# V's seven products in another order, with their gate words on VectorE and x's combination back on SyncE's queue

## The chip, the cores and the metric

The kernel runs on one core of one Trainium2 chip. What is measured is the device time of one execution in microseconds (us). Five engines work side by side, each through its own list of instructions in order: TensorE (PE, matrix products; PEld are its weight loads), VectorE (DVE), ScalarE (ACT), GpSimd (POOL) and SyncE (SP, which here only issues transfers). Transfers between the chip's main memory (HBM) and the on-chip memory (SBUF) can be issued by SyncE, ScalarE or GpSimd and are carried out by 16 DMA engines. TensorE adds its results up in PSUM, which has 8 banks. An engine that needs another's result waits at the head of its list, and everything behind it in that list waits too.

## The reference

One decoder block with 512 tokens and 2048 features: a norm, one wide input projection, attention in two groups of heads, an output projection, and a last norm. What matters here is the projection of the values of group A and of the 24 gate columns:

```python
h = _rmsnorm(x, norm_g[l])
proj = h @ w_in[l]
(qa, kca, vca, ksa, vsa, kwa, vwa, za, ga,
 qb, kb, vb, zb) = jnp.split(proj, offsets, axis=-1)
...
kc = _compress(_rope(_heads(kca, N_KV_A, HEAD_DIM_A)), cmp_k_pos[l], cmp_k_w1[l], cmp_k_w2[l])
vc = _compress(_heads(vca, N_KV_A, HEAD_DIM_A), cmp_v_pos[l], cmp_v_w1[l], cmp_v_w2[l])
...
o_sel = _selected_attention(qa, _rope(_heads(ksa, N_KV_A, HEAD_DIM_A)), _heads(vsa, N_KV_A, HEAD_DIM_A), sel_idx)
o_win = _banded_attention(qa, _rope(_heads(kwa, N_KV_A, HEAD_DIM_A)), _heads(vwa, N_KV_A, HEAD_DIM_A), WIN_A)
gates = jax.nn.sigmoid(ga.astype(jnp.float32)).reshape(B, S, N_KV_A, GROUP_A, 3).astype(x.dtype)
```

`vsa` and `vwa` are 256 columns each: together they are what the kernel calls V. `_compress` squeezes blocks of 32 tokens through two small matrices, once for keys and once for values.

## The kernel before

**Words.** Products are taken in a fast 32-bit format that keeps fewer bits. So every operand is split in two words: ScalarE copies it into the high word, VectorE subtracts that from the source to get the low word (`split`, lines 541 and 542). A product of two split operands is three matmuls (`mm3`, lines 119 to 121). The words of weights lie in three rotating buffers (`words`, tags `whi` and `wlo`), so VectorE and ScalarE can be at most three buffers ahead of TensorE.

**Seven products.** x is cut in even and odd blocks of 128 features and in tokens 0 to 255 and 256 to 511; the weights of V in four quarters (0: `vsa` of the even blocks, 1: `vwa` of the even, 2: `vsa` of the odd, 3: `vwa` of the odd). The 2 by 2 block product is then formed with seven products instead of eight, by combinations of x and sums of quarters. Their names and the weights that each uses are: 22 (quarter 3), p (quarter 0), 21 (quarter 1), 12 (quarter 0 + quarter 2), u (quarter 0 + 2 + 3), w (quarter 2 + 3), q (all four). A quarter is held in two halves (g = 0, 1) of 128 x 1024 numbers, 512 KB. The sums are made in place: p's tiles become those of 12, then u, then q; w's own tiles get quarter 3 added.

Of x's combinations, those for p, u and q are kept in SBUF as words (`pu`, `qw`). The one for w is built earlier, written to HBM (`wd`) and brought back over the even blocks of x's first 256 tokens (`even`, lines 825 to 827), four transfers of 512 KB that may start once the last projection before the stage (`proj(wz[19])`) has read those blocks. Only product w reads them; 12 and 22 read the odd blocks, 21 the even blocks of the other tokens.

**The stage.** The order is 22, p, 21, 12, u, w, q. Four of the products are `wide` (22, p, 21, 12): beside 256 value columns they carry the 24 gate columns, whose weights are split too, for two blocks at a time: ScalarE makes the high gate word (line 839), GpSimd the low one (line 840). One wide product is 8 blocks x 2 groups of 128 tokens x 3 matmuls of 280 columns. The other three are `narrow`, with 256 columns. 22 and 21 share one pair of PSUM banks, p and 12 another, u and q a third bank, w a fourth; `vd` and `vj` gather them on VectorE.

Between the halves of these products stand the 16 units of the compression's first matrix (`compress_unit`, line 686 on; 0 to 7 for keys, 8 to 15 for values). Each loads two halves of 256 KB (`cw`, line 696, SyncE's queue) into four small tiles, splits them, and takes 8 matmuls. So SyncE's queue holds the cw loads, the quarters of V, and the first quarters of the stage behind it: `keys(1)`, which takes seven products of the same kind for a pair of keys. Its quarter 0 goes to tile `raw3`, quarter 2 to `raw1` (with quarter 3 added to it by an accumulating transfer on GpSimd, line 907), quarter 3 and the sum of 0 and 2 to the two tiles `quarters` (named `ahead` in the profile), in which 21 and then w lay before, and quarter 1 to `raw2`. Quarter 1 of V is added into u's tiles to make q's by accumulating transfers on GpSimd too (line 910).

`v_words` turns finished rows of V into words: ScalarE's copies, GpSimd's subtractions, and a transfer to HBM on GpSimd's queue. Its small tile `other` uses the slot `pcr`, in which `gw[0]`, one of the two gate weights, lies before.

**What sets the order.** The program text gives priorities; a planner with its own estimate of each instruction's duration takes, for each engine, the earliest instruction in the text that it holds to be ready. The list it writes is fixed. `tc.issue_after(i)` keeps what is inside it behind instruction i on i's engine.

## Time and profile before

| | us |
|---|---|
| median of 3 timed runs | 824.88 |
| lowest and highest of them | 821.97 and 828.35 |
| the profiled execution | 826.33 |
| its span, from the first to the last instruction | 824.5 |
| mean granted TensorE clock in it | 0.986 |

The page gives for each engine its busy time, and the span in 40 slices with the busy share in tenths. A row of the windows view has the window and its length in us, then for each engine the busy time and the number of instructions, then the TensorE clock that was granted (1.00 is full speed), the mean busy share of the 16 DMA engines, and GB/s. A row of the timeline has the start and the duration in us, the engine (SPq is SyncE's queue), the line, the operation with result<-sources and shape, and how many were merged; in brackets is how long the engine stood idle before it and who ended that. A group's row has busy time, mean ns of one, and the idle time before them.

### The profile page before, as it was taken

Reading aid. Unit: us, or ns where it says so; the run is one execution under the profiler, and the core shown is the slowest. Engines: PE = TensorE matmul, PEld = TensorE weight load, DVE = VectorE, ACT = ScalarE, POOL = GpSimd, SP = SyncE. Lnnn points to the kernel's source line nnn. Section 1 sums busy time; section 2 is a strip of 40 time slices with the busy share of each in tenths; the row PEclk is TensorE's granted clock in tenths of the full one; section 3 lists DMA queues with packets and bytes.
Section 4 is the critical chain, followed back from the end, with each engine's and each line's share of the span. In section 5 each row is a group of like instructions: output and inputs, shape, how many; then the busy total and the mean of one; then the engine's idle time right before and its main releaser. Section 6 shows DMA issues by size and latency. Waiting matters only on the chain.

```text
span 824.5 us, 15301 instructions
## 1 busy us (share of the span) xinstructions
PE 797.6 (97%) x5644; PEld 742.4 (90%) x5644; DVE 699.9 (85%) x1399; ACT 512.5 (62%) x1108; POOL 123.6 (15%) x132
## 2 busy tenths in 40 slices
PE   9999999999999969889999999999999999999996
PEld 8887888888888859779999999999999999999996
DVE  7668979988898857856999999998999798977895
ACT  6636656756666436455445796868687877554555
POOL 4515001111011013422111101110100000010000
PEclk9999999999999979989999999999999999999999
DMA  7562144456455465794752232244033935797845
GB/s 245 173 228 91 67 149 133 149 142 193 149 157 167 153 210 175 198 262 119 205 162 70 78 116 69 65 151 132 27 112 119 368 116 205 255 260 182 238 114 204
DMA packets 49595, 132.08 MB, mean 160 GB/s; under 512 B 6033, under 2 KB 9137, under 8 KB 49521
## 3 DMA queue, kind: packets, MB, share of 16 engines
q1 hardware_dynamic: 43088, 110.89, 40.3%
q0 software_dynamic: 6144, 19.70, 10.6%
q8 instruction: 44, 0.72, 0.4%
q10 hardware_dynamic: 288, 0.52, 0.2%
q14 instruction: 31, 0.25, 0.1%
HBM read 114.28 MB, written 16.81 MB: 159 GB/s over the span
## 4 chain that ended last, share of the span: by engine, by line
PE 42%; DVE 9%; DMA 6%; issue 5%; ACT 2%; POOL 0%; POOLq 0%; ACTq 0%; DVEq 0%
PE pj L121 8%; PE pj L119 8%; PE pj L120 7%; PE sp L984 4%; PE oa L120 2%; PE oa L121 2%; PE oa L119 2%; DVE wlo L542 2%; DMA cw<-cw 2%; DMA rw<-wos 2%; DMA ch<-wos 2%; PE tp L1021 2%; PE bank L120 1%; DVE wlo L1104 1%; PE op L1027 1%
## 5 line engine op out<-in xcount | busy, mean ns | idle before, releaser
L119 PE MATMUL pj<-xh,whi 128*128 128x256 f32 (+1 forms) x592 | 197.2, 333 | 0.1
L121 PE MATMUL pj<-xh,wlo 128*128 128x256 f32 (+1 forms) x592 | 196.6, 332 | 0.3 <-DVE wlo L542 0.3
L120 PE MATMUL pj<-xl,whi 128*128 128x256 f32 (+1 forms) x592 | 196.6, 332 | 0.0
L121 PEld LDWEIGHTS pj<-xh,wlo 128*128 128x128 f32 x592 | 111.6, 188 | 10.6 <-DVE wlo L542 0.6
L119 PEld LDWEIGHTS pj<-xh,whi 128*128 128x128 f32 x592 | 111.4, 188 | 10.7 <-ACT t L607 0.5
L120 PEld LDWEIGHTS pj<-xl,whi 128*128 128x128 f32 x592 | 111.4, 188 | 9.6
L541 ACT ACTIVATE whi<-raw 128x1024 fp32r<-128x1024 f32 (+1 forms) x82 | 80.2, 993 | 39.1 <-DVE raw L580 11.6
L542 DVE TENSOR_TENSOR wlo<-raw,whi 128x1024 fp32r<-128x1024 f32 (+1 forms) x82 | 95.9, 1182 | 6.0 <-ACT whi L541 5.6
L99 DVE TENSOR_TENSOR wlo<-raw,whi 128x1024 fp32r<-128x1024 f32 (+1 forms) x60 | 71.4, 1191 | 16.4 <-ACT whi L97 15.9
L97 ACT ACTIVATE whi<-raw 128x1024 fp32r<-128x1024 f32 (+1 forms) x59 | 55.5, 943 | 24.4 <-PE pj L120 13.6
L120 PE MATMUL oa<-wlo,xh 128*128 128x256 f32 x200 | 55.6, 278 | 0.0
L119 PE MATMUL oa<-whi,xh 128*128 128x256 f32 x200 | 55.5, 278 | 0.0
L121 PE MATMUL oa<-whi,xl 128*128 128x256 f32 x200 | 55.3, 277 | 0.0
L121 PE MATMUL pj<-pu,wlo 128*128 128x256 f32 x160 | 45.2, 283 | 0.7 <-DVE wlo L542 0.7
L119 PE MATMUL pj<-pu,whi 128*128 128x256 f32 x160 | 45.3, 283 | 0.0
L120 PE MATMUL pj<-pu,whi 128*128 128x256 f32 x160 | 44.8, 280 | 0.0
L288 ACT ACTIVATE ph<-tp 128x512 fp32r<-128x512 f32 (+1 forms) x64 | 34.2, 562 | 15.2 <-PE tp L384 7.5
L289 DVE TENSOR_TENSOR pl<-tp,ph 128x512 fp32r<-128x512 f32 (+1 forms) x64 | 40.7, 649 | 0.9 <-ACT ph L288 0.7
L121 PEld LDWEIGHTS oa<-whi,xl 128*128 128x128 f32 x200 | 37.6, 188 | 0.0
L120 PEld LDWEIGHTS oa<-wlo,xh 128*128 128x128 f32 x200 | 37.6, 188 | 0.0
L119 PEld LDWEIGHTS oa<-whi,xh 128*128 128x128 f32 x200 | 37.5, 188 | 0.0
L363 ACT ACTIVATE ttb<-ttb,sums 128x256 f32<-128x256 f32 (+1 forms) x64 | 30.0, 471 | 10.8 <-DVE sums L356 10.8
(428 smaller groups left out, 2398.6 us busy)
## 6 DMA issues: line engine op xcount, KB each, us to landing
raw<-wq SPq DMA_DIRECT2D x41, 512.0 KB, 4.0
raw<-wz SPq DMA_DIRECT2D x36, 512.0 KB, 3.7
cw<-cw SPq DMA_DIRECT2D x32, 256.0 KB, 3.7
raw<-wos SPq DMA_DIRECT2D x14, 512.0 KB, 5.8
rw<-wos SPq DMA_DIRECT2D x10, 512.0 KB, 5.4
xr<-xT SPq DMA_DIRECT2D x16, 256.0 KB, 3.6
rows<-xT SPq DMA_DIRECT2D x8, 512.0 KB, 4.4
raw<-wo SPq DMA_DIRECT2D x8, 512.0 KB, 5.8
```

Source lines behind the costliest of these rows:

```text
L97: last["hi"] = act.activation(hi[:, :width], rw[:, :width], AF.Copy).ins
L99: last["lo"] = dve.tensor_tensor(out=lo[:, :width], in0=rw[:, :width], in1=hi[:, :width].bitcast(F32), op=ALU.subtract).ins
L119: pe.matmul(ps, ah, bh, start=first, stop=False, skip_group_check=go_on)
L120: pe.matmul(ps, ah, bl, start=False, stop=False, skip_group_check=go_on)
L121: recent["mm"] = pe.matmul(ps, al, bh, start=False, stop=last, skip_group_check=go_on).ins
L288: act.activation(ph, tp, AF.Copy)
L289: dve.tensor_tensor(out=pl, in0=tp, in1=ph.bitcast(F32), op=ALU.subtract)
L363: act.activation(tv, tv, AF.Exp, bias=mn[:, e, v:v + 1], scale=-1.0, accum_out=dn[:, e, v:v + 1])
L541: split_hi = act.activation(hi, src, AF.Copy).ins
L542: last["lo"] = dve.tensor_tensor(out=lo, in0=src, in1=hi.bitcast(F32), op=ALU.subtract).ins
L984: pe.matmul(sp[:, a:b], qq[:, qs], kk[:, ko:ko + b - a], start=pi == 0, stop=pi == 2)
L1021: pe.transpose(tp[:, e * 256 + i * P:e * 256 + i * P + P], views[2 * i + w][2][:, kt * P:(kt + 1) * P], ident)
```

## The change

The order of the products becomes 22, p, 12, u, 21, w, q. w is loaded into `quarters` at the start, where 21 was; 21 is loaded later, into 22's tiles, once u's and w's sums have read them. The sums for 12 stand behind p, those for u and w behind 12. The two pairs of banks are swapped. The units are spread anew: 6 and 7 in u, 8 and 9 in 21, 10 to 13 in w; 14 and 15 stay in q. The low gate words and the sum of the gate weights go from GpSimd to VectorE. The four transfers that bring x's combination back go from GpSimd's queue to SyncE's, behind p's and w's loads in the text. Of the key pair's quarters, 0 now comes into 22's tile after 21; quarter 2, its accumulate, and the sum stand behind the load of quarter 3, which follows w, and quarter 1 after them.

```diff
-    for ms in (slice(0, 4), slice(4, 8)):
-        for e in range(2):
-            pool.dma_start(even[e][:, ms], wd[e, :, ms])
-    pair22, pair11 = [bank(4), bank(5)], [bank(0), bank(1)]
+    pair22, pair11 = [bank(0), bank(1)], [bank(4), bank(5)]
...
-                pool.tensor_tensor(out=gl, in0=gate[:, m:m + 2, :], in1=gh.bitcast(F32), op=ALU.subtract)
+                dve.tensor_tensor(out=gl, in0=gate[:, m:m + 2, :], in1=gh.bitcast(F32), op=ALU.subtract)
...
     for g in range(2):
-        load_half("21", 1, g, quarters[g])
+        load_half("w", 2, g, quarters[g])
+        raw_of["12", g] = raw_of["u", g] = raw_of["q", g] = raw_of["p", g]
+    for ms in (slice(0, 4), slice(4, 8)):
+        for e in range(2):
+            nc.sync.dma_start(even[e][:, ms], wd[e, :, ms])
     wide("22", pair22, True, gw[1], {0: units(0), 1: units(1)})
...
-    pool.tensor_tensor(out=gw[1], in0=gw[1], in1=gw[0], op=ALU.add)
+    dve.tensor_tensor(out=gw[1], in0=gw[1], in1=gw[0], op=ALU.add)
     wide("p", pair11, True, gw[0], {0: units(2), 1: units(3)})
+    for g in range(2):
+        add(raw_of["12", g], raw_of["12", g], raw_of["w", g])
     for t in range(2):
         add(vd[:, t], vd[:, t], pair11[t][:, 0:256])
-    wide("21", pair22, False, gw[0], {0: units(4), 1: units(5)})
+    wide("12", pair11, False, gw[1], {0: units(4), 1: units(5)})
+    for g in range(2):
+        add(raw_of["u", g], raw_of["u", g], raw_of["22", g])
+        add(raw_of["w", g], raw_of["w", g], raw_of["22", g])
+        load_half("21", 1, g, raw_of["22", g])
...
+    narrow("u", bx, True, {0: units(6), 1: units(7)})
+    for g in range(2):
+        pool.dma_start(raw_of["q", g], wv[1, g], accum_op=ALU.add)
+    add(vd, vd, bx.rearrange("p (t c) -> p t c", c=256))
+    csum = compress_sum(cacc[0])
+    cacc[1] = bank(4)
+    wide("21", pair22, False, gw[0], {0: units(8), 1: units(9)})
+    k0w = compressed_keys(csum)
+    early.append(load_quarter(wq[0], tags[0], 0))
...
-    narrow("w", bc, True, {0: units(11, 12), 1: units(13)})
+    narrow("w", bc, True, {0: units(10, 11), 1: units(12, 13)})
+    last["dma"] = nc.sync.dma_start(early[0], wq[0][3]).ins
     add(vd, vd, bc.rearrange("p (t c) -> p t c", c=256))
-    last["dma"] = nc.sync.dma_start(early[0], wq[0][3]).ins
-    sums(*ready, wq[0], 0, 2)
     for t in range(2):
         v_words(0, 2 + t, vd[:, t])
     narrow("q", bx, False, {0: units(14), 1: units(15)})
-    early.append(load_quarter(wq[0], tags[3], 1))
+    with tc.issue_after(last["dma"]):
+        sums(*ready, wq[0], 0, 2)
+        early.append(load_quarter(wq[0], tags[2], 2))
+        added.append(early[2])
+        pool.dma_start(early[2], wq[0][3], accum_op=ALU.add)
+        early.append(load_quarter(wq[0], tags[3], 1))
```

More of the change, by code (lines that the diff above doesn't have):

```diff
@@ L875, in hybrid_block @@
         act.activation(vd[:, t], pair22[t][:, 0:256], AF.Copy, scale=-1.0)
-    pool.tensor_tensor(out=gw[1], in0=gw[1], in1=gw[0], op=ALU.add)
+    dve.tensor_tensor(out=gw[1], in0=gw[1], in1=gw[0], op=ALU.add)
     wide("p", pair11, True, gw[0], {0: units(2), 1: units(3)})
+    for g in range(2):
+        add(raw_of["12", g], raw_of["12", g], raw_of["w", g])
     for t in range(2):
         add(vd[:, t], vd[:, t], pair11[t][:, 0:256])
-    wide("21", pair22, False, gw[0], {0: units(4), 1: units(5)})
-    for t in range(2):
-        add(vj[:, t], vd[:, t], pair22[t][:, 0:256])
+    wide("12", pair11, False, gw[1], {0: units(4), 1: units(5)})
[3 more added lines that the diff above has]
+        load_half("21", 1, g, raw_of["22", g])
+    for t in range(2):
+        add(vj[:, t], vd[:, t], pair11[t][:, 0:256], ALU.subtract)
+    for t in range(2):
+        dve.tensor_scalar(gates[:, t, :], pair11[t][:, 256:280], rstd[:, t:t + 1], None, op0=ALU.mult)
+        v_words(0, t, pair11[t][:, 0:256])
+    narrow("u", bx, True, {0: units(6), 1: units(7)})
[7 more added lines that the diff above has]
+    early.append(load_quarter(wq[0], tags[0], 0))
+    for t in range(2):
+        add(vj[:, t], vj[:, t], pair22[t][:, 0:256])
     for t in range(2):
@@ L885, in hybrid_block @@
         v_words(1, 2 + t, pair22[t][:, 0:256])
-    for g in range(2):
-        load_half("w", 2, g, quarters[g])
-        raw_of["12", g] = raw_of["p", g]
-        add(raw_of["12", g], raw_of["12", g], raw_of["w", g])
-        add(raw_of["w", g], raw_of["w", g], raw_of["22", g])
-    wide("12", pair11, False, gw[1], {0: units(6), 1: units(7)})
-    for t in range(2):
-        add(vj[:, t], vj[:, t], pair11[t][:, 0:256], ALU.subtract)
-    for t in range(2):
-        dve.tensor_scalar(gates[:, t, :], pair11[t][:, 256:280], rstd[:, t:t + 1], None, op0=ALU.mult)
-        v_words(0, t, pair11[t][:, 0:256])
-    csum = compress_sum(cacc[0])
-    cacc[1] = bank(4)
-    for g in range(2):
-        raw_of["u", g] = raw_of["p", g]
-        add(raw_of["u", g], raw_of["u", g], raw_of["22", g])
-    narrow("u", bx, True, {0: units(8, 9), 1: units(10)})
-    k0w = compressed_keys(csum)
-    early.append(load_quarter(wq[0], tags[0], 0))
-    early.append(load_quarter(wq[0], tags[2], 2))
-    added.append(early[2])
-    pool.dma_start(early[2], wq[0][3], accum_op=ALU.add)
-    for g in range(2):
-        raw_of["q", g] = raw_of["p", g]
-        pool.dma_start(raw_of["q", g], wv[1, g], accum_op=ALU.add)
-    add(vd, vd, bx.rearrange("p (t c) -> p t c", c=256))
-    narrow("w", bc, True, {0: units(11, 12), 1: units(13)})
+    narrow("w", bc, True, {0: units(10, 11), 1: units(12, 13)})
+    last["dma"] = nc.sync.dma_start(early[0], wq[0][3]).ins
     add(vd, vd, bc.rearrange("p (t c) -> p t c", c=256))
-    last["dma"] = nc.sync.dma_start(early[0], wq[0][3]).ins
-    sums(*ready, wq[0], 0, 2)
     for t in range(2):
```

## The prediction

> **What bounds the kernel now.** I read the page first, for the engine that fills the span and for the slices in which it doesn't.
>
> ```profile
> span 824.5 us, 15301 instructions
> ...
> PE 797.6 (97%) x5644; PEld 742.4 (90%) x5644; DVE 699.9 (85%) x1399; ACT 512.5 (62%) x1108; POOL 123.6 (15%) x132
> ...
> PEclk9999999999999979989999999999999999999999
> ```
>
> TensorE is busy for 97% of the span, so a change pays only where TensorE waits or where its clock is cut. One slice is 824.5 / 40 = 20.6 us. The digits of the clock fall below 9 in the 15th (289 to 309 us) and the 18th (350 to 371) alone: both lie in the stage of V's seven products, which the change rewrites. The windows view of that stage, cut where TensorE stops and where its clock changes, with two windows behind it for comparison:
>
> ```profile
> core 0: us, PE busy (x) PEld busy (x) DVE busy (x) ACT busy (x) POOL busy (x), PEclk, DMA share, GB/s
> 291.64:296.31 4.67, 4.38 (x31) 3.85 (x29) 4.55 (x22) 3.48 (x12) 0.53 (x2) 1.00 0.94 288
> 296.31:303.73 7.42, 0.01 (x2) 0.00 (x1) 2.22 (x5) 0.70 (x2) 1.88 (x4) 0.68 0.66 221
> 303.73:309.18 5.45, 5.45 (x23) 5.45 (x24) 1.29 (x2) 1.54 (x3) 0.77 (x2) 0.50 0.35 108
> 312.00:320.00 8.00, 8.00 (x66) 8.00 (x65) 6.04 (x13) 4.91 (x13) 2.43 (x4) 1.00 0.45 132
> 331.60:336.56 4.96, 1.88 (x11) 1.41 (x11) 4.96 (x7) 2.43 (x5) 3.11 (x5) 0.99 0.55 144
> 336.56:339.90 3.34, 3.34 (x14) 3.34 (x15) 2.79 (x4) 0.58 (x1) 0.04 (x1) 0.50 0.73 232
> 351.54:353.58 2.04, 0.00 (x0) 0.00 (x1) 0.02 (x1) 0.68 (x2) 1.57 (x2) 0.99 1.05 284
> 353.58:360.38 6.80, 6.61 (x27) 6.02 (x28) 4.77 (x8) 3.12 (x8) 2.67 (x4) 0.50 0.98 227
> 340.00:360.00 20.00, 17.21 (x113) 16.05 (x113) 12.44 (x25) 9.36 (x23) 8.84 (x12) 0.84 1.00 245
> 380.00:390.00 10.00, 9.80 (x84) 9.59 (x82) 4.56 (x8) 4.88 (x11) 3.46 (x6) 1.00 0.22 74
> 400.00:420.00 20.00, 19.67 (x171) 19.31 (x170) 19.59 (x28) 9.17 (x12) 3.62 (x5) 1.00 0.62 178
> ```
>
> There are three losses, each a stop and then a stretch in which TensorE is full and gets half its clock. **A:** 7.42 us empty and 5.45 us at 0.50, which costs 5.45 / 2 = 2.7. **C**, between the third and fourth product: 4.96 - 1.88 = 3.1 us empty and 3.34 us at 0.50, which costs 1.7. **D**, after the fifth: 2.04 us empty and 6.80 us at 0.50, which costs 3.4. Together 10.1 + 4.8 + 5.4 = 20.3 us. Behind the stage (from 380 us) TensorE is busy for 98% at full clock, so time saved in the stage should reach the end. A shorter stop that left the clock alone lies early in the kernel:
>
> ```profile
> 73.17:74.72 1.55, 0.00 (x0) 0.03 (x1) 1.42 (x3) 1.51 (x3) 0.00 (x0) 1.00 0.00 0
> 74.72:79.00 4.28, 4.28 (x25) 3.79 (x26) 3.50 (x7) 3.27 (x5) 2.72 (x2) 1.00 0.31 112
> ```
>
> So the point from which a stop also costs clock lies here between 1.55 and 2.04 us. Three rows of the timeline mark the stage: the last matmul of product 22, the first of u, and the first of the keys, which ends it.
>
> ```profile
> 308.80 0.43 PE L121 MATMUL bank<-whi,xl 128*128 128x280 f32 x1
> ...
> 341.80 0.29 PE L119 MATMUL bank<-whi,pu 128*128 128x256 f32 x1
> ...
> 376.51 0.28 PE L119 MATMUL pj<-xh,whi 128*128 128x256 f32 x1
> ```
>
> The timeline tells whom loss A waits for:
>
> ```profile
> 291.73 0.45 POOL L840 TENSOR_TENSOR wlo<-gw,whi 128x48 fp32r<-128x48 f32 x1
> ...
> 292.04 8.34 SPq L696 DMA_DIRECT2D cw<-cw  x3
> ...
> 296.57 1.27 DVE L542 TENSOR_TENSOR wlo<-raw,whi 128x512 fp32r<-128x512 f32 x2
> 298.07 0.77 POOL L827 DMA_DIRECT2D xl<-wd  x1 [5.89 <-issue]
> 298.66 0.63 ACT L541 ACTIVATE whi<-cw 128x512 fp32r<-128x512 f32 x1 [2.28 <-DMA cw<-cw]
> ...
> 302.61 0.76 POOL L827 DMA_DIRECT2D xh<-wd  x1 [3.77 <-issue]
> 303.38 0.53 POOL L840 TENSOR_TENSOR wlo<-gw,whi 128x48 fp32r<-128x48 f32 x2
> ...
> 303.73 0.60 PE L120 MATMUL bank<-wlo,xh 128*128 128x280 f32 x1 [7.42 <-POOL wlo L840]
> ```
>
> Product 22 waits for the low gate words (L840). They are 0.5 us of work, but stand in POOL's queue behind x's combination (L827), whose last two issues stand 5.89 and 3.77 us before they go. The 256 value columns of the same units were ready at 296.57 + 1.27 = 297.84.
>
> **The change part by part.** The sum is made against the profiled execution's 826.33 us (span 824.5); the median of the three timed runs is 824.88 (821.97 to 828.35), 1.4 below it.
>
> *First gap.* Gate words on VectorE and the combination on SyncE's queue both take L840 out from behind L827. What is late next is VectorE: of the two splits at 296.57 the first ends at about 297.2, its gate word about 0.2 later, so TensorE resumes near 297.5 and 1.2 us of 7.42 are left: **-6.2**. If both splits and gate words come first, 1.9 are left (-5.5); if VectorE's planner puts them before its earlier work, none (-7.4).
>
> *Clock behind it.* 1.2 us is under the 1.55 that left the clock alone: **-2.7**. At 1.9 us one stretch like C's 3.34 would stay at half clock: -1.0.
>
> *The combination on SyncE.* Four transfers of 512 KB now stand on the queue of the cw loads. The first two wait for the last projection's first half alone; the other two would start near 291.4, beside the 1 MB of w which takes the place of 21's 1 MB. The second half of compression unit 0 arrived at 298.6 (ACT's wait for DMA), with SyncE's issue at 292.04. 1 MB more at the 288 GB/s of the first window would put it at 302.2; half of that megabyte was there before too. TensorE reaches that unit at 296.31 + 1.2 + 2.7 = 300.2, with 1.3 us of splitting ahead of it. From 0 to 3.3; I take the end near the present arrival, **+0.5**.
>
> *Order 22, p, 12, u, 21, w, q.* Loss C first:
>
> ```profile
> 325.26 0.33 SPq L809 DMA_DIRECT2D ahead<-wv  x1
> ...
> 330.40 1.23 DVE L867 TENSOR_TENSOR raw<-raw,ahead 128x1024 f32<-128x1024 f32 x1 [0.57 <-DMA ahead<-wv]
> ...
> 333.28 1.30 DVE L867 TENSOR_TENSOR raw<-raw 128x1024 f32<-128x1024 f32 x1
> 334.51 1.30 DVE L867 TENSOR_TENSOR ahead<-ahead,raw 128x1024 f32<-128x1024 f32 x1
> ...
> 336.56 0.57 PE L120 MATMUL bank<-wlo,xh 128*128 128x280 f32 x1 [1.54 <-DVE wlo L542]
> ```
>
> w can only be loaded once 21's splits have left its tiles, so its sums come late, and the splits of 12 stand behind them on VectorE, busy for 4.96 of 4.96 us. In the new order w lies in its own tiles from the start, so p + w needs no load; two of the sums move into product p. But u's and w's sums, four of 1.2 to 1.3 us, now fall into 12, and what is queued behind them is 12's and u's own splits. I leave two of them exposed, 2.8 us with some clock, of C's 4.8: **-2.0**. Ends: nothing left (-4.8), or two more exposed (+2.5).
>
> Loss D is a DMA's:
>
> ```profile
> 352.90 0.63 ACT L541 ACTIVATE whi<-cw 128x512 fp32r<-128x512 f32 x1 [6.11 <-DMA cw<-cw]
> ```
> ```profile
> DMA to landing us min/median/max: 2.6/3.6/9.2
> ```
>
> A cw half that takes 3.6 us as a rule took up to 9.2 while the DMA share was 1.00 (340 to 360). In that time the key pair's quarter 2 and its accumulate (1 MB) were moved too; the change sends them behind w's last use. 21's megabyte comes in instead, behind the sums that free 22's tiles, and u hides it: u with its units took from 341.80 to the stop at 351.54, 9.7 us. I leave 1.5 of D's 5.4: **-3.9**. Ends: -5.4, or 21's load itself at 9.2 us, 5.6 more than the median and no cover left: about +3.6. The later quarters are needed in the keys' third, fourth and sixth product, when the share is 0.22 (380 to 390): no cost.
>
> ```profile
> raw<-wv POOLq DMA_DIRECT2D x2, 512.0 KB, 8.6
> ahead<-wv SPq DMA_DIRECT2D x4, 512.0 KB, 4.6
> ```
>
> POOL's accumulates for q take 8.6 us each and are wanted at the last product; u, whose words they overwrite, is now three products earlier: free.
>
> *Gate words on VectorE.*
>
> ```profile
> L840 POOL TENSOR_TENSOR wlo<-gw,whi 128x48 fp32r<-128x48 f32 x16 | 9.7, 612 | 39.0 <-ACT whi L839 39.0
> L521 DVE TENSOR_TENSOR posw<-pos,posw 128x64 fp32r<-128x64 f32 x1 | 0.2, 228 | 0.1
> ```
>
> 16 of them at 0.23 (a slightly larger one on VectorE) are 3.7 us, and the gate sum at most 0.4. In 312 to 320 VectorE idles 1.96 of 8 us, so the four of a product (0.9) fit; in 12, full with sums, they don't: **+1.0**, between 0 and 4.1.
>
> *Banks* of the two pairs are swapped; the compressions' bank 4 is free after 12, earlier than it is used: 0.
>
> Sum: -6.2 - 2.7 + 0.5 - 2.0 - 3.9 + 1.0 = -13.3, so 813.0 for an execution like the profiled one and **811.6**, say 811.5, as a median. All good ends: -7.4 - 2.7 - 4.8 - 5.4 = -20.3, 804.6. All bad ends: -5.5 - 1.0 + 3.3 + 2.5 + 3.6 + 4.1 = +7.0, 831.9, but they would have to come together.
>
> **The rivals.** *Only the first gap is won.* The stage has the same sums, splits and nearly the same bytes in less time; VectorE (4.96 of 4.96) or the DMA engines (1.00) take over, and C and D reappear elsewhere: -6.2 - 2.7 + 0.5 + 1.0 = -7.4, 817.5. For it speak these two rows, against it that two sums, a load that 12 waited for and 1 MB leave the crowded places.
>
> *All three losses go:* 804.6. VectorE's idle time in 312 to 320 speaks for it, the four sums in one product against it.
>
> *The cw half behind the combination.* If all 2 MB are issued ahead of it in one queue, unit 0 comes at 302.2 and later, costs 3.3 and a half-clock stretch of 1.7 instead of 0.5: -8.8, 816. The Trainium skill's "DMA: Bandwidth & Descriptors", "Queues, rings and completion order", speaks for this one: the engines take turns between queues, packet by packet, so the combination on POOL's queue let the cw load through, and on SyncE's it goes first. The row at 292.04 against 298.66, 6.6 us for a cw load, shows that turns were no full cure before either.
>
> *Slower: SyncE's queue becomes the bound.* From 12 on it holds five loads that wait for another engine to free their tiles: 21's halves, the key pair's quarter 0, quarter 3 and the sum. Behind each stand cw halves. If each lets TensorE run dry as in D, it costs 5.4; five make 27.0 in place of C and D's 10.2, and with the first gap -7.4 + 16.8 = +9.4: 834. It decides from the fourth on. Against it: before, SyncE also had such waits (325.26 is one) and only two stops came of them. By "TensorE: Matmul & The Clock Gate" in the Trainium skill, Part 1, the clock falls after an idle stretch of about 3.4 us; by that a 2.04 us stop would cost itself alone, five would make 10.2, and this rival would not be slower. The measured 0.50 behind 2.04 us says otherwise, and I go by it.
>
> **How the numbers follow.** Chances: the forecast 0.46 (807 to 816), only the first gap 0.27 (815 to 822), all three 0.13 (803 to 807), the cw half 0.07, SyncE's queue 0.07. A median of a few runs of this kernel can tell about 1%, 8.2 us, from no change. Faster than 816.6: 0.44 + 0.13 + 0.04 + 0.06 = 0.67. Slower than 833.1: 0.05. Within: 0.28. The range from 803 to 822 leaves out SyncE's queue, the worst of the second case and a little below, under 2 in 10.
>
> **What would show it.** L840 is listed under VectorE and no wait of TensorE names POOL; the first product ends near 301 and not 308.8 us, with the clock at 1.00 behind it: steps one and two. The first compression unit waits for DMA by under 1 us: step three. Between 12 and u TensorE waits for VectorE by 2 to 3 us: C's step. No cw half of the stage takes over 6 us, and 21's splits don't wait for their load: D's. V's stage ends near 363 instead of 376.5. The prediction is wrong if the first product still stops for over 2 us, if half-clock stretches appear elsewhere, or if the keys' products wait for a quarter that is now loaded later.

## The result, and the profile after

The changed kernel takes **816.84 us** as the median of 4 runs (815.45 to 817.88); the kernel before, run beside it, 825.35 us (821.97 to 828.35, 4 runs). The ratio is 0.9897, with a 95% interval of 0.9854 to 0.9940: faster by 1.0%, or 8.5 us, where the forecast of 811.5 lies 13.85 below this median. Six further runs of the same kernel in a later comparison gave 818.43 us and 0.9904 [0.9871, 0.9937]. The profiled execution took 817.78 us, 8.6 less than the one of before.

The page of the changed kernel, for the lines that were read first before:

```profile
span 815.6 us, 15253 instructions
...
PE 795.2 (97%) x5644; PEld 739.7 (91%) x5644; DVE 700.5 (86%) x1416; ACT 512.6 (63%) x1108; POOL 110.1 (13%) x111
...
PEclk9999999999999999989999999999999999999998
...
cw<-cw SPq DMA_DIRECT2D x32, 256.0 KB, 3.5
```

TensorE's busy time fell by 2.4 us (from 797.6), the span by 8.9: most of the gain is time in which TensorE no longer stands still. Of the two dips in the clock, the one in the 15th slice (loss A) has gone and the one in the 18th has stayed.

The windows view of the stage, in the order of time (window and length, busy us of each engine with its instructions, granted clock, DMA share, GB/s):

```profile
291.65:296.06 4.41, 4.22 (x31) 3.79 (x29) 4.41 (x21) 3.52 (x12) 0.00 (x0) 1.00 0.93 305
296.06:297.33 1.27, 0.00 (x0) 0.00 (x1) 1.27 (x5) 0.05 (x1) 0.00 (x0) 1.00 1.07 370
297.33:300.43 3.10, 3.10 (x22) 2.87 (x22) 1.86 (x5) 1.48 (x3) 0.00 (x0) 1.00 0.94 330
300.43:302.18 1.75, 0.39 (x2) 0.19 (x2) 1.15 (x2) 1.47 (x5) 0.00 (x0) 1.00 0.43 114
322.50:366.20 43.70, 39.97 (x279) 37.99 (x279) 28.92 (x57) 24.55 (x54) 15.19 (x19) 0.88 0.87 247
333.08:336.50 3.42, 1.73 (x13) 1.44 (x12) 0.86 (x3) 1.60 (x5) 0.00 (x0) 1.00 0.89 340
336.50:339.91 3.41, 3.41 (x17) 3.41 (x16) 2.93 (x9) 2.00 (x6) 1.88 (x2) 0.50 0.63 148
346.74:350.15 3.41, 2.21 (x9) 1.39 (x9) 2.72 (x9) 3.41 (x10) 2.45 (x5) 1.00 0.77 258
350.15:356.98 6.83, 6.47 (x29) 6.05 (x29) 4.01 (x8) 2.53 (x6) 2.23 (x3) 0.50 0.74 210
```

Loss A is now 1.27 us empty, with full clock behind it in this execution. The first product ends at 300.43, and 1.4 us more are lost at the first compression unit (300.43 to 302.18). From 322.50 on (u, 21, w, q) the DMA engines are 0.87 busy on the average, and two stretches at half clock, 3.41 and 6.83 us long, have taken the place of C's and D's.

The rows of the timeline that answer to those shown before (the low gate word's line is now L837, three lines further up):

```profile
297.09 0.19 DVE L837 TENSOR_TENSOR wlo<-gw,whi 128x48 fp32r<-128x48 f32 x1
...
297.33 0.40 PE L120 MATMUL bank<-wlo,xh 128*128 128x280 f32 x1 [1.27 <-DVE wlo L837]
...
300.77 0.63 ACT L541 ACTIVATE whi<-cw 128x512 fp32r<-128x512 f32 x1 [0.28 <-DMA cw<-cw]
...
335.58 0.38 PE L702 MATMUL bank<-whi,kvw 128*128 128x256 f32 x1 [1.69 <-ACT whi L541]
...
366.25 0.28 PE L119 MATMUL pj<-xh,whi 128*128 128x256 f32 x1
...
372.14 0.31 ACT L503 ACTIVATE v<-vt 128x128 fp32r<-128x128 f32 x1 [3.36 <-DMA Vd<-v]
...
372.98 0.38 PE L119 MATMUL pj<-xh,whi 128*128 128x256 f32 x1 [0.72 <-ACT t L607]
```

The stage's end, the first matmul of the keys, moved from 376.51 to 366.25. From TensorE's stop in product 22 to that matmul it took 376.51 - 296.31 = 80.20 us and now takes 366.25 - 296.06 = 70.19: **10.0 us less in the stage**. What follows the stage took 824.5 - 376.51 = 448.0 us and now takes 815.6 - 366.25 = 449.4: **1.4 us are given back in the keys**, where TensorE waits for ScalarE (372.98), and ScalarE had stood 3.36 us in front of one row of V, whose small tile was still being read by an earlier transfer to `Vd` (372.14). The page's chain of work that ended last now names that transfer among its lines; before, it did not:

```profile
PE pj L119 12%; PE pj L121 12%; PE pj L120 12%; PE oa L120 5%; PE oa L121 5%; PE oa L119 5%; PE sp L983 4%; DVE wlo L542 3%; DMA yw<-st 2%; DMA cw<-cw 2%; DVE wlo L99 2%; PE tp L1020 2%; DMA Vd<-v 1%; PE bank L121 1%; PE bank L120 1%
```

### The profile page after: what moved, and what is told of

It reads as the page before. It is cut to its first block, busy times and chain, and to the rows that moved or that the text cites. A ratio compares the mean times of both kernels' runs of the same rounds, so it can differ in the third digit from the quotient of the medians.

```text
span 815.6 us, 15253 instructions
## 1 busy us (share of the span) xinstructions
PE 795.2 (97%) x5644; PEld 739.7 (91%) x5644; DVE 700.5 (86%) x1416; ACT 512.6 (63%) x1108; POOL 110.1 (13%) x111
## 4 chain that ended last, share of the span: by engine, by line
PE 68%; DVE 15%; DMA 9%; issue 4%; ACT 3%; POOL 1%; SPq 1%; DVEq 0%; POOLq 0%; ACTq 0%
PE pj L119 12%; PE pj L121 12%; PE pj L120 12%; PE oa L120 5%; PE oa L121 5%; PE oa L119 5%; PE sp L983 4%; DVE wlo L542 3%; DMA yw<-st 2%; DMA cw<-cw 2%; DVE wlo L99 2%; PE tp L1020 2%; DMA Vd<-v 1%; PE bank L121 1%; PE bank L120 1%
## 5 line engine op out<-in xcount | busy, mean ns | idle before, releaser
L541 ACT ACTIVATE whi<-raw 128x1024 fp32r<-128x1024 f32 (+1 forms) x86 | 82.7, 976 | 40.6 <-PE bank L121 12.7
L542 DVE TENSOR_TENSOR wlo<-raw,whi 128x1024 fp32r<-128x1024 f32 (+1 forms) x86 | 98.4, 1155 | 3.8 <-ACT whi L541 3.2
L99 DVE TENSOR_TENSOR wlo<-raw,whi 128x1024 fp32r<-128x1024 f32 (+1 forms) x60 | 71.8, 1198 | 13.5 <-ACT whi L97 13.1
L97 ACT ACTIVATE whi<-raw 128x1024 fp32r<-128x1024 f32 (+1 forms) x59 | 55.5, 944 | 22.9 <-PE pj L120 13.4
```

The source lines that it names most:

```text
L97: last["hi"] = act.activation(hi[:, :width], rw[:, :width], AF.Copy).ins
L99: last["lo"] = dve.tensor_tensor(out=lo[:, :width], in0=rw[:, :width], in1=hi[:, :width].bitcast(F32), op=ALU.subtract).ins
L541: split_hi = act.activation(hi, src, AF.Copy).ins
L542: last["lo"] = dve.tensor_tensor(out=lo, in0=src, in1=hi.bitcast(F32), op=ALU.subtract).ins
```

## The experiments

The theory after the result had three parts. Each of the two moves out of GpSimd's queue (gate words, combination) is enough to end loss A. What the moves win is lost again in the second half of the stage, unless the order is changed too. And from u on the DMA engines, not one transfer, set the pace. The rivals are named with each run. In the table "stage end" is the start of the keys' first matmul, "rest" the span minus it, and "row wait" the time that ScalarE stood before L503 for a transfer to `Vd`, from 320 us to the stage's end and from there to 392 us. Medians and ratios are over all runs, the last four columns are one profiled execution each. Ratios are to the kernel before, run beside each. The changed kernel's own two profiles differ by 2.6 us in the stage's end, so a difference of that size in this column shows nothing by itself.

| kernel | median us (runs) | ratio, 95% interval | stage end | rest | row wait in the stage | row wait in the keys |
|---|---|---|---|---|---|---|
| before, profiled | 825.35 (4) | 1 | 376.51 | 448.0 | 0 | 1.4 |
| changed, profiled | 816.84 (4) | 0.9897 [0.9854, 0.9940] | 366.25 | 449.4 | 0.8 | 5.1 |
| changed, later comparison | 818.43 (6) | 0.9904 [0.9871, 0.9937] | 363.66 | 449.3 | 1.7 | 4.2 |
| 1 gate words alone | 820.30 (6) | 0.9925 [0.9897, 0.9952] | 370.36 | 448.8 | 1.8 | 1.3 |
| 2 combination alone | 820.09 (6) | 0.9925 [0.9900, 0.9949] | 369.45 | 447.3 | 0 | 1.3 |
| 3 both, old order | 822.83 (10) | 0.9967 [0.9947, 0.9986] | 369.44 | 448.8 | 8.0 | 1.4 |
| 4 q's quarter added later | 820.32 (5) | 0.9927 [0.9901, 0.9953] | 370.59 | 448.6 | 1.5 | 3.1 |
| 5 without q's quarter | 816.20 (2) | 0.9875 [0.9823, 0.9927] | 364.22 | 451.7 | 1.2 | 6.3 |
| 6 keys' sum later | 817.00 (6) | 0.9878 [0.9845, 0.9911] | 362.56 | 452.1 | 3.1 | 6.1 |
| 7 slots exchanged | 816.37 (6) | 0.9884 [0.9846, 0.9923] | 363.20 | 452.4 | 5.3 | 7.6 |
| 8 both of 6 and 7 | 816.79 (4) | 0.9876 [0.9827, 0.9924] | 364.70 | 454.3 | 4.6 | 6.2 |
| 9 cw loads halved | 819.24 (4) | 0.9898 [0.9860, 0.9935] | 365.17 | 449.0 | 3.2 | 4.6 |
| 10 later quarters undone | 816.83 (4) | 0.9868 [0.9829, 0.9908] | 368.34 | 447.1 | 0 | 1.6 |
| 11 gate words undone | 820.24 (6) | 0.9907 [0.9871, 0.9943] | 362.85 | 451.7 | 3.9 | 6.3 |

**1 and 2: one move alone, in the old order.** Both start from the kernel before. The first:

```diff
-                pool.tensor_tensor(out=gl, in0=gate[:, m:m + 2, :], in1=gh.bitcast(F32), op=ALU.subtract)
+                dve.tensor_tensor(out=gl, in0=gate[:, m:m + 2, :], in1=gh.bitcast(F32), op=ALU.subtract)
...
-    pool.tensor_tensor(out=gw[1], in0=gw[1], in1=gw[0], op=ALU.add)
+    dve.tensor_tensor(out=gw[1], in0=gw[1], in1=gw[0], op=ALU.add)
```

> The kernel before, with only the low gate words and the gate sum on VectorE; the combination stays on GpSimd's queue and the order stays. My theory: loss A goes as it went in the changed kernel (first stop from 7.4 to about 1.3 us, no half-clock stretch behind it), C (3.1 us empty and one half-clock stretch) and D (2.0 us and two) stay: 825.3 - 8.5 = about 817, as fast as the whole change. Rival: the new order brought the gain, and this alone leaves it above 821.

The second moves the combination's four transfers to SyncE's queue, behind 21's loads:

```diff
-    for ms in (slice(0, 4), slice(4, 8)):
-        for e in range(2):
-            pool.dma_start(even[e][:, ms], wd[e, :, ms])
...
+    for ms in (slice(0, 4), slice(4, 8)):
+        for e in range(2):
+            nc.sync.dma_start(even[e][:, ms], wd[e, :, ms])
     wide("22", pair22, True, gw[1], {0: units(0), 1: units(1)})
```

> The kernel before, with only x's combination moved to SyncE's queue; gate words stay on GpSimd. My theory: GpSimd is free when the gate words come, so loss A goes here too; the cw half of unit 0 comes about 2 us later than before behind the combination, a stop of about 1 us: 817 to 818. Rival: gate words on GpSimd cost by themselves (0.6 us each, in turn with ScalarE) and keep 2 us or more of the first stop: 819 or more.

The timeline of the kernel with the gate words alone, at the first stop and at the longest one of the second half:

```profile
298.21 0.39 PE L120 MATMUL bank<-wlo,xh 128*128 128x280 f32 x1 [1.14 <-DVE wlo L840]
...
347.15 0.38 PE L702 MATMUL bank<-whi,kvw 128*128 128x256 f32 x1 [1.99 <-ACT whi L541]
```

And of the kernel with the combination alone:

```profile
299.14 0.40 PE L120 MATMUL bank<-wlo,xh 128*128 128x280 f32 x1 [1.75 <-POOL wlo L837]
...
346.70 0.58 PE L702 MATMUL bank<-whi,kvw 128*128 128x256 f32 x1 [3.41 <-ACT whi L541]
```

Either move turns the 7.42 us stop into one of 1.1 to 1.8 us, so the two are two cures for one wait, and their gains don't add. Each gives some 6 us of 826 (both medians 820), less than the 817 and 817 to 818 that were expected; for the second move that is the time its rival gave (819 or more). With the gate words alone a stretch of 3.41 us at half clock still follows the first stop (298.79 to 302.21), against the expectation. The stop by a cw half in the second half of the stage is there in both, with 1.99 and 3.41 us, as D was before with 2.04.

**3: both moves, in the old order.** The two diffs above together.

> The changed kernel's gate words on VectorE and combination on SyncE, in the order and with the loads of before. It tells what the new order is worth. My theory: about 817, the same as the changed kernel: the order saves C's 4.8 us and pays as much for cw halves that collide with q's accumulates. Rival 1: the order is worth 3 us or more, 820. Rival 2: the order costs, 814 or less.

822.83 us: less gain than one move alone, by 2.5 to 2.7 us, and the intervals overlap only at their ends (0.9947 to 0.9986 against 0.9897 to 0.9952 and 0.9900 to 0.9949). The first rival of the expectation (the order is worth 3 us or more) held. The timeline of this kernel has two long stops in the second half:

```profile
339.70 0.31 ACT L503 ACTIVATE v<-vt 128x128 fp32r<-128x128 f32 x1 [3.19 <-DMA Vd<-v]
...
341.21 0.43 PE L119 MATMUL bank<-whi,pu 128*128 128x256 f32 x1 [2.71 <-ACT whi L541]
...
356.59 0.39 PE L702 MATMUL bank<-whi,kvw 128*128 128x256 f32 x1 [2.87 <-ACT whi L541]
```

Both are waits for a copy of ScalarE's: the first copy stood behind a row of V, for which ScalarE had waited 3.19 us, the second waited 2.63 us for a cw half. But this profiled execution (820.01 us) is the fastest of the kernel's ten and lies between those of 1 and 2 (821.01 and 818.50), so where the median's 2.5 to 2.7 us go is not shown. The changed kernel differs from this one by the order, with its loads and units, and is 4.4 to 6 us faster (818.43 and 816.84 against 822.83; 0.9904 [0.9871, 0.9937] against 0.9967 [0.9947, 0.9986]). So with both moves made the new order is worth these 4.4 to 6 us, which the prediction's first rival (only the first gap is won) denied.

In the old order's second half, from u on, the DMA engines were busy for 0.95 of the time already; the window of the kernel before:

```profile
341.80:376.50 34.70, 30.91 (x218) 28.70 (x217) 22.19 (x41) 18.96 (x39) 11.34 (x15) 0.90 0.95 261
```

and of the kernel with both moves:

```profile
332.80:369.40 36.60, 29.55 (x218) 28.24 (x217) 21.64 (x43) 19.13 (x39) 13.25 (x19) 0.91 0.93 263
```

It began 9 us earlier and took 1.9 us longer, with the DMA engines 0.93 busy in place of 0.95.

**4: the changed kernel with q's quarter added later.** Its accumulating transfers are issued behind the first row of 12, in the hope that the two cw halves that end the stop at 335.58 come sooner.

```diff
-        pool.dma_start(Vd[:, :, t, w].rearrange("e p c -> p e c"), other.bitcast(F32))
+        return pool.dma_start(Vd[:, :, t, w].rearrange("e p c -> p e c"), other.bitcast(F32)).ins
...
-        v_words(0, t, pair11[t][:, 0:256])
+        rows_out = v_words(0, t, pair11[t][:, 0:256])
+        first_rows_out = rows_out if t == 0 else first_rows_out
...
-    for g in range(2):
-        pool.dma_start(raw_of["q", g], wv[1, g], accum_op=ALU.add)
+    with tc.issue_after(first_rows_out):
+        for g in range(2):
+            pool.dma_start(raw_of["q", g], wv[1, g], accum_op=ALU.add)
```

> The changed kernel, with q's two accumulates behind the transfer of the first rows of V on GpSimd, which puts them about 15 us later (from 323 and 326 to 340 us). My theory: with them away the cw halves of units 8 and 9 land in about 4 us instead of 8 to 10, the stop of 1.7 us at 334 and the half-clock stretch from 336.5 go: 816.8 - 3.4 = 813.5, if q's words are still there in time (they land near 349, wanted near 356). Rival: the loads are late because 21's megabyte and the fifth sum fill the engines, and the stop stays: 816 to 818.

The transfers that this aims at, as the DMA view of the changed kernel lists them between 320 and 331 us (KB each, median us to landing):

```profile
cw<-cw SPq DMA_DIRECT2D x5, 256.0 KB, 8.2
raw<-wv POOLq DMA_DIRECT2D x2, 512.0 KB, 8.3
```

Beside the two accumulates the cw halves take 8.2 us, against 3.5 for all 32 of them on the page. The four issued from 323.9 to 327.8, which units 8 and 9 in product 21 need, by their line's own view:

```profile
DMA to landing us min/median/max: 7.7/8.2/10.4
```

The same four, in this kernel with the accumulates later and then in that of 5 without them:

```profile
DMA to landing us min/median/max: 2.6/3.0/3.5
```

```profile
DMA to landing us min/median/max: 2.6/2.8/2.9
```

So it is the accumulates that make these loads slow. That they make the stop at 334 is less sure: it is gone with the accumulates later, but in the changed kernel's second profile it is absent as well, with the accumulates in place and the four loads at 7.1 to 8.2 us. Two other stops stand in w and q (timeline of the kernel with the accumulates later):

```profile
346.75 0.39 PE L702 MATMUL bank<-whi,kvw 128*128 128x256 f32 x1 [2.12 <-ACT whi L541]
...
365.66 0.39 PE L702 MATMUL bank<-whi,kvw 128*128 128x256 f32 x1 [1.94 <-ACT whi L541]
```

The first waits for a cw half, for which ScalarE had stood 4.91 us, now beside the accumulates at 340; the second stands behind a row of V (1.50 us, until 364.78). The stage ends 4.3 us later (370.59), with 820.32 us as the median, where 813.5 was expected.

**5: the changed kernel without q's added quarter.** The two accumulating transfers are left out: q uses its weights without quarter 1, and 1 MB of transfers is missing.

```diff
-    for g in range(2):
-        pool.dma_start(raw_of["q", g], wv[1, g], accum_op=ALU.add)
```

> The changed kernel without the two accumulates that add quarter 1 to q's weights; that addition is left out, so q is formed with u's weights. It shows what these two cost. My theory: 2 accumulates of 8.3 us are the largest single share of the engines' time between 323 and 335; without them no cw half there takes over 6 us, the stop at 334 and its half-clock stretch go (3.4 us) and part of w's: the stage ends 4 to 6 us earlier, near 361. Rival: the engines are busy with other transfers all the same (share 0.8 and more), and the stage ends within 2 us of the changed kernel's.

The stop at 334 is absent here too. The stage ends 2.0 us earlier, the bound of the rival and not the 4 to 6 us of the theory, and the rest takes 2.3 us longer (451.7). Its timeline shows where:

```profile
345.93 0.38 PE L702 MATMUL bank<-whi,kvw 128*128 128x256 f32 x1 [1.54 <-ACT whi L541]
...
372.19 0.39 PE L119 MATMUL pj<-xh,whi 128*128 128x256 f32 x1 [1.97 <-ACT t L607]
```

The stop in w remains with 1.54 us, and the one in the keys has grown from 0.72 to 1.97. With two runs, 816.20 us can't be told from the changed kernel.

**6 to 8: two small edits on the side of the keys.** The keys' sum of quarters (L770 and its accumulate L771, issued at 330.6 in the middle of the crowd) is held behind the quarters (`behind_quarters` is the last of their loads); the small tile of V's rows is given the slot of the gate weight that is free earlier; then both.

```diff
         t = fifth(1)
-        sums(t, wq[1 - g], 0, 2)
+        with tc.issue_after(behind_quarters):
+            sums(t, wq[1 - g], 0, 2)
```

> The changed kernel, with the load and the accumulate of the second key pair's sum (the fifth tile, 512 KB each, now issued at 331 and 338 us) behind the key pair's last quarter at 362 us. My theory, formed after the first four: from product u on the stage is bound by the DMA engines (44 us at a share of 0.87), so an order only moves the stops, and taking work out shortens it. The fifth sum is about 6 us of their time; the stops of 1.7 us at 334 and of w (346 to 351) shrink, with one of the two half-clock stretches: 3 to 5 us faster than the changed kernel, 812 to 814. Rival: q's accumulates alone make the stops, the fifth sum is later than the first of them, and nothing is won: within 1.5 us of the changed kernel.

```diff
-    gw = [wk.tile([P, 8, 24], F32, name="gw", tag=tag, bufs=1) for tag in ("pcr", "pd")]
+    gw = [wk.tile([P, 8, 24], F32, name="gw", tag=tag, bufs=1) for tag in ("pd", "pcr")]
```

> The changed kernel, with the two gate weights' slots exchanged, so that the slot in which v_words puts its second words is free after product 12 and not only after 21's gate words. My theory: two of the six transfers of V's rows go some 15 us earlier, the copies that stood behind them on ScalarE in the keys' first product don't wait (3.4 us at 372), and the keys' stops of 0.7 and 1.2 us go: 1.5 to 2 us faster. Rival: the chain of six transfers is set by its last two, which come from vj at the stage's end, and nothing is won.

> The two edits that each gained at most 0.5 us, together: the sum for the keys issued behind the quarters, and the two gate weights' slots exchanged, so that the rows' small tile no longer waits for the gate weights of 21. If the keys give back what the stage saves through that slot, both together gain more than each, 2 to 3 us: 814 to 815. Rival (the stage's saving is given back by whatever transfers are then late): within 1 us of the changed kernel, 816 to 818.

817.00, 816.37 and 816.79 us: none can be told from the changed kernel, so the gains expected of the first two (to 812 to 814, and by 1.5 to 2 us) did not come. All three end the stage earlier than the changed kernel's first profile (362.56, 363.20 and 364.70 against 366.25; 363.66 in its second), and in all three the rest takes 2.7 to 5.0 us longer. In the timeline of the kernel with exchanged slots, and then of the one with both edits, the keys show it:

```profile
372.44 0.58 PE L119 MATMUL pj<-xh,whi 128*128 128x256 f32 x1 [3.24 <-ACT t L607]
```

```profile
379.51 0.38 PE L119 MATMUL pj<-pu,whi 128*128 128x256 f32 x1 [3.10 <-ACT whi L541]
```

The slot that is free earlier did not shorten the waits for V's rows: ScalarE stands 5.34 us for one at 331.70 and 5.88 us at 371.61, where the changed kernel's longest wait was 3.36. The rival of the last expectation held for the total: the edits don't add up.

**9: the changed kernel with half of the cw bytes.** The units 8 to 15 load half as much and use that half twice; the other half of the second compression's weights is left out.

```diff
-            last["dma"] = nc.sync.dma_start(r, cw1[:, b, u, half * S:half * S + S]).ins
+            n = 256 if b else S
+            last["dma"] = nc.sync.dma_start(r[:, 0:n], cw1[:, b, u, half * S:half * S + n]).ins
+            if b:
+                r = r[:, 0:256].unsqueeze(1).to_broadcast([P, 2, 256])
...
-                  r.rearrange("p (j c) -> p j c", c=256))
+                  r if b else r.rearrange("p (j c) -> p j c", c=256))
```

> The changed kernel, in which the units 8 to 15 of the compression load only the first half of each cw tile (128 KB in place of 256 KB) and use that half twice, with the same shapes on every engine; half of the second compression's weights are so left out of the computation. From 21 on 2 MB less come in, some 8 us of transfers at the 248 GB/s measured from u to the stage's end. Theory (from u on the DMA engines bind): no unit waits over 0.5 us for its cw, the second half-clock stretch (6.8 us) is gone or halved, and the stage ends 4 to 7 us earlier, near 360; if the keys give back what was saved in the stage, the total gains only 2 to 5 us: 812 to 815. Rival (the order of issue, or VectorE, binds): cw halves still take 6 us and more behind q's added quarter, stops of 1.5 to 2 us stay, the stage ends within 1.5 us of 366.3.

The windows view of this kernel from u on:

```profile
324.40:365.10 40.70, 36.20 (x281) 35.20 (x280) 29.42 (x57) 24.84 (x54) 14.36 (x19) 0.96 0.79 215
```

40.70 x 215 GB/s is 8.8 MB, 2 MB less than the 43.70 x 247 = 10.8 MB of the changed kernel. The stage ended at 365.17, 1.1 us earlier, and the total is no better (819.24, where 812 to 815 was expected). From u's first matmul to the keys' it took 40.9 us; the changed kernel's two profiles took 44.2 and 41.4. ScalarE's waits for cw halves between 322 and 366 us did fall, to 1.3 us from 4.9 and 6.0, but with 2 MB less neither the stage nor the total gained what the theory of the DMA engines' throughput asks for. Two views show what stood in its place. The DMA view between 324 and 331 us, beside q's accumulates:

```profile
raw<-wv POOLq DMA_DIRECT2D x2, 512.0 KB, 7.9
cw<-cw SPq DMA_DIRECT2D x4, 128.0 KB, 7.1
```

Half the bytes, and still 7.1 us in place of 8.2 (7.6 in the changed kernel's second profile): beside the accumulates a cw half waits for what was in flight before it, not for its own bytes. And the timeline at the longest stop:

```profile
347.58 0.31 ACT L503 ACTIVATE v<-VF 128x128 fp32r<-128x128 f32 x1 [3.16 <-DMA Vd<-v]
...
348.56 1.04 ACT L541 ACTIVATE whi<-ahead 128x1024 fp32r<-128x1024 f32 x1
...
349.66 0.38 PE L119 MATMUL bank<-whi,xh 128*128 128x256 f32 x1 [3.35 <-ACT whi L541]
```

TensorE stands 3.35 us for the high word of w's second half. That copy (L541 at 348.56) went as soon as ScalarE came to it; it stood in ScalarE's list behind a row of V (L503), which waited 3.16 us for a transfer to `Vd` to leave the rows' one small tile.

**10: the later quarters undone.** Quarter 2 of the keys, its accumulate and the sum go back to where they were, right behind quarter 0.

```diff
     early.append(load_quarter(wq[0], tags[0], 0))
+    early.append(load_quarter(wq[0], tags[2], 2))
+    added.append(early[2])
+    pool.dma_start(early[2], wq[0][3], accum_op=ALU.add)
...
     last["dma"] = nc.sync.dma_start(early[0], wq[0][3]).ins
+    sums(*ready, wq[0], 0, 2)
...
-    with tc.issue_after(last["dma"]):
-        sums(*ready, wq[0], 0, 2)
-        early.append(load_quarter(wq[0], tags[2], 2))
-        added.append(early[2])
-        pool.dma_start(early[2], wq[0][3], accum_op=ALU.add)
-        early.append(load_quarter(wq[0], tags[3], 1))
+    early.append(load_quarter(wq[0], tags[3], 1))
```

> The changed kernel with the key pair's quarter 2 and its accumulate put back right behind quarter 0, behind 21, and the sum with no order of its own, as before the change. Theory (from u on the DMA engines bind): 1 MB more falls into w, 4 us of transfers at 248 GB/s; one more stop of 2 to 3 us in w or q, stage end 2 to 4 us later than 366.3, total 819 to 822. Rival (single transfers only shift the stops, and what the stage loses the keys give back): stage end within 1.5 us, total within 1.5 us of the changed kernel's 816.8 to 818.4.

One more stop in q, in the timeline of this kernel:

```profile
363.42 0.39 PE L702 MATMUL bank<-whi,kvw 128*128 128x256 f32 x1 [2.76 <-ACT whi L541]
```

The stage ends 2.1 us later, within the theory's 2 to 4, but the rest takes 447.1, the least of all, and the total is the rival's: 816.83. Loading the quarters later is worth nothing that can be measured.

**11: the gate words undone, in the new order.** GpSimd makes them again; the combination stays on SyncE's queue.

> The changed kernel with the gate words and the gate sum back on GpSimd: the new order and the combination on SyncE's queue stay. Theory: with the combination off GpSimd's queue L840 no longer stands behind it in 22, p and 12; in 21 it stands behind the accumulates for q and the rows of 12, whose issues held GpSimd for up to 5.9 us before, so a stop of 2 to 5 us at the head of 21 (near 324): 818 to 822. Rival (GpSimd's issues no longer wait, and VectorE, which was full in 12, is relieved of 3.7 us): no stop at 21, total 814 to 817.

The theory's stop in 21 came, between its halves and shorter than the 2 to 5 us expected (timeline):

```profile
338.56 0.39 PE L120 MATMUL bank<-wlo,xh 128*128 128x280 f32 x1 [1.29 <-POOL wlo L837]
```

The median, 820.24 (814.91 to 822.20), can't be told from the changed kernel's 816.84 and 818.43, since the intervals overlap almost wholly (0.9871 to 0.9943). So neither a gain nor a cost of VectorE's gate words is shown once the combination has left GpSimd's queue: the new order with one of the two moves can't be told from that with both.

**Where the rest comes from.** In the table the rest follows ScalarE's wait for V's rows in the keys, behind the stage's end: 447.1 to 448.8 us where it waits 1.3 to 1.6 us, 448.6 to 449.4 where it waits 3.1 to 5.1, and 451.7 to 454.3 where it waits 6.1 to 7.6. The waits in the stage do not count here: both moves in the old order have 8.0 us of them, 1.4 in the keys, and a rest of 448.8. Part of the longest rests is clock: in 5, 6 and 7 a stretch of 3.41 us at half clock, and in 8 one of 6.83, stands between the stage's end and 392 us; in the changed kernel's two profiles and in 11 none does. The waits view from the stage's end to 392 us (total, times, longest) of the kernel with the later quarters undone, and of the one with exchanged slots:

```profile
ACT v L503 <- DMA Vd<-v: 1.6, 1, 1.6
```

```profile
ACT v L503 <- DMA Vd<-v: 7.6, 2, 5.9
```

That this wait takes back what the stage saves is argued from these rows and from the one at 372.14, not shown by an edit: a second tile for the rows, which would take the wait away, was not tried.

## Why the prediction was right, and where it was not

The time lies in the range, and the sign is the one forecast, by a gain just over the 1% bound. But it lies in the part that the prediction gave to its rival *only the first gap* (815 to 822, chance 0.27), not in the forecast's own (807 to 816, 0.46): the sum was 4.4 us too good (-13.3 against -8.9 of the span). A sign of being wrong came, too, half-clock stretches elsewhere (336.50 and 350.15), and a sign of D's step failed: cw halves took over 6 us. Step by step, from the first profile:

- **First gap, -6.2:** 7.42 to 1.27, -6.15, and what is late next is what was named, VectorE: its gate word at 297.09, which TensorE's stop ends on (297.33; 297.5 was forecast). Right.
- **Clock behind it, -2.7:** clock 1.00 at 297.33 to 300.43. Right in this execution, and by luck: in the changed kernel's second profile a first stop of 1.19 us is followed by one of 1.40 at the first compression unit, and then by 3.41 us at half clock (302.45 to 305.87), which leaves -1.0. The reason given was wrong (below).
- **The combination on SyncE, +0.5 between 0 and 3.3:** the second half of unit 0 came at 300.77 and TensorE stood 1.36 us (300.43 to 302.18 with 0.39 busy) where before no stop of 0.25 us or more stood at this place: about +1.4. In the bounds, mis-sized by 0.9. The sign given, a wait for DMA of under 1 us, was met (0.28 at 300.77), but was no measure of it: TensorE also stands for the copy itself (0.63) and for VectorE's low word behind it (0.34).
- **Loss C, leave 2.8:** C lay inside the fourth product, 12 (first matmul at 327.21, u's at 341.80), and not ahead of it, as the prediction puts it; that changes no term. Between 12 and u TensorE now stops 0.30 us. With two stops of 0.60 behind a unit's copy in p and 12, one of which was there before as well, at most 1.5 us are left of 4.8: -3.3 where -2.0 was forecast. The fear that four sums would crowd VectorE in product 12 was too great.
- **Loss D, leave 1.5: this step failed.** Four stops (1.69, 0.57, 0.34, 0.34) and two stretches at half clock (3.41 and 6.83 us, so 5.1 us) make 2.94 + 5.1 = 8.1 us; counted the same way, the second half had D's 5.4 and four stops of 0.26 to 0.36 before, 6.7. Not -3.9, but +1.4; the second profile, with 2.1 us of stops and one stretch of 6.83, gives -1.2, so the size hangs on the execution, but neither comes near. The step's sentence that 21's megabyte comes in hidden behind u was right. What it blamed for D, quarter 2 of the keys and its accumulate, gains nothing that can be measured by coming later (10).
- **"Free" for q's accumulates was the error inside it.** They were costed by their own due time (the last product) and not by what they hold up: 1 MB, at 8.3 us each, with the cw halves of units 8 and 9 beside them at 7.7 to 10.4 us. In the kernel before they stood in D's stretch, too (issued at 342.86 and 352.42). Without them these loads take 2.6 to 3.5 us (4 and 5). What the delay costs in all stays open: neither moving them nor leaving them out made the kernel measurably faster.
- **Later quarters, no cost:** no cost, and no gain either (10). The keys' products do not wait for a quarter, as forecast; they wait for ScalarE behind V's rows (372.14 and 372.98), which the prediction did not list.
- **Gate words on VectorE, +1.0:** no stop in the stage longer than 0.34 us behind VectorE from p on, and 11 shows no difference: nearer to 0.
- **Behind the stage, 0:** +1.4. The sentence "time saved in the stage should reach the end" held for 86% of it here, and for less in 5 to 8.

With stops under 0.25 us left aside, -6.15 - 2.7 + 1.4 - 3.3 + 1.4 = -9.4 of the stage's -10.0. The stage's -10.0, 1.4 from the keys and -0.25 from before the stage make the span's -8.9.

Two rivals lie within 1 us of 816.84. *Only the first gap is won* gives 817.5, but its mechanism was half wrong: C did not come back, and the two moves without the new order give 822.8 (3). Its other half, D reappearing in the crowded second half, is what happened. *The cw half behind the combination* gives 816 for a stop of 3.3 us and a half-clock stretch at unit 0; the stop was 1.4 us, and the stretch came in the second of its two profiles alone. *SyncE's queue becomes the bound* did not come: no stop of TensorE in the stage over 1.69 us.

**The point from which a stop costs clock** was the other error. The prediction put it between 1.55 and 2.04 us for a single stop. In the changed kernel a stop of 1.69 us cost a stretch, and three of 0.57, 0.34 and 0.34 us cost 6.83 us at half clock; with the combination alone 1.75 us cost none. What fits is told in the last section.

## What to carry to other kernels

Where two things stand in one queue and one of them is late, either can be moved, and the second move need not pay: here both together gained less than one in the old order (3), and in the new order the second shows no gain (11). Cost a transfer by what is issued right behind and beside it, not by when its own data are due: here two accumulates with three products to spare made the loads beside them 8 us long instead of 3. And follow an in-order engine's list behind each thing that can stand at its head: a row of V, waiting for the one small tile, held up the words that TensorE was waiting for (3.35 us at 349.66 in 9).

## What the runs showed of the hardware

**The clock is decided every 3.41 us.** In the 14 profiles all the stretches at half clock between 290 and 392 us are whole multiples of 3.41 us long, and within one profile they start at whole multiples of 3.413 us from one another: in the changed kernel at 336.50 and 350.15 (4 steps), with the cw loads halved at 303.46 and 351.25 (14 steps), with both edits of 8 at 304.70, 338.83 and 379.79 (10 and 12 steps). In the kernel before, A's stretch began at 298.94, before TensorE had resumed. The 3.41 us ahead of each of its three half-clock stretches:

```profile
295.53:298.94 3.41, 0.78 (x6) 0.46 (x4) 2.31 (x6) 1.13 (x5) 0.77 (x1) 1.00 0.87 329
333.07:336.49 3.42, 1.35 (x8) 0.85 (x7) 3.42 (x5) 1.15 (x2) 1.64 (x3) 1.00 0.79 207
350.14:353.55 3.41, 1.39 (x13) 1.25 (x11) 0.00 (x0) 0.65 (x2) 1.70 (x2) 1.00 1.05 317
```

In the changed kernel they are the rows at 333.08 and 346.74 shown above: 13 and 9 matmuls, in 1.73 and 2.21 us. The profile of the kernel with the gate words undone has no half clock there, though it stopped 1.73 us at 296.24; the two steps of its own grid that share this stop:

```profile
293.50:296.92 3.42, 2.36 (x16) 1.85 (x14) 3.26 (x20) 2.82 (x11) 1.13 (x1) 1.00 0.94 345
296.92:300.33 3.41, 2.36 (x18) 2.36 (x19) 0.90 (x3) 0.72 (x2) 1.84 (x3) 1.00 0.89 311
```

Each half of the stop leaves 16 and 18 matmuls in its step, and nothing is lost. So two stops of nearly the same length, 1.73 and 1.69 us, cost nothing and 1.7 us more, by where they fall on a grid that lies differently in each execution. The changed kernel's two profiles show it for the same place: behind the first stop and that at unit 0 the clock held in one (the step there, 298.96 to 302.37, has 14 matmuls in 2.05 us) and fell in the other, after this step:

```profile
299.04:302.45 3.41, 1.67 (x12) 1.32 (x11) 2.11 (x5) 2.35 (x7) 0.00 (x0) 1.00 0.58 190
302.45:305.87 3.42, 3.42 (x17) 3.42 (x16) 3.34 (x8) 1.44 (x4) 0.00 (x0) 0.50 0.23 68
```

In these steps at most 13 matmuls stand ahead of a fall, and 16 or 18 where none followed; a limit between them is fitted to the rows, not tested, and in other profiles single steps near it went either way (14 matmuls in 2.01 us at 294.89 in 4, and the clock fell; 13 in 2.14 us at 347.88 in 10, and it did not). The Trainium skill's "TensorE: Matmul & The Clock Gate", Part 1, gives a window of 3413 ns that runs freely, and the grid here agrees with that; it lets the clock fall after at least one idle window, and there the measurement differs: a step with TensorE idle for 1.2 of 3.41 us, in three stops, was enough (346.74). This also bears on how far the runs of one kernel lie apart: the changed kernel's ten runs reach from 815.15 to 821.19 us, so single profiles that differ by 2 or 3 us say little about an edit.

**Half the bytes, the same time.** cw halves of 128 KB issued beside two accumulating transfers took 7.1 us, those of 256 KB 8.2 and 7.6, and those of 256 KB with no accumulate beside them 3.0 and 2.8 (medians of four each).
